# Merge gates of a gated two-branch block by Strassen's products, in a stage ahead of attention

## The chip, the core and the metric

The kernel runs on one core of a Trainium2 chip. The metric is device time in microseconds (us). The engines are called as in the profile: PE (TensorE matmul; PEld its weight loads), DVE (VectorE), ACT (ScalarE), POOL (GpSimd), SP (SyncE, whose queue issues the DMAs).

## The reference

One layer of a streaming encoder on 1024 tokens of width 1024. Everything is float32. Cut to what matters here:

```python
h = rms_norm(x, norm_w) * (1 + scale) + shift
(cq, ckv, k_rope, gate_a, q_b, k_b, v_b, f_b, gate_b,
 mg_a, mg_b) = split(h @ w_in)             # mg_a, mg_b: 1024 columns each
o_a = mla_attention(...)                   # 8 heads, from cq, ckv, k_rope
o_b = fox_attention(...)                   # 8 heads, from q_b, k_b, v_b, f_b
y_a, y_b = o_a * silu(gate_a), o_b * silu(gate_b)
merged = sigmoid(mg_a) * (y_a @ w_branch_a) + sigmoid(mg_b) * (y_b @ w_branch_b)
out = x + gate * (merged @ w_out)
```

## The kernel before

Float32 products are made of three float32r products: each operand is split into a high part (a rounding copy on ACT, L115) and a low part (the rest, a subtraction on DVE, L116), and high x high, high x low and low x high are summed in PSUM. `hT_hi` and `hT_lo` hold h, transposed: 8 tiles of 128 columns by 1024 tokens.

In order of time: phase 0 (h, and the latent cq), latents, the operands of branch A (`g2q`, `g2k`), attention over 16 heads (8 of branch A, 8 of branch B), the branch products, the output product. The order of every engine is the order in which the program emits its instructions; nothing reorders them, so an instruction that waits holds up all behind it on its engine.

Work that only has to be done in time is a generator, `fillers`, from which other stages draw some matmuls at a time with `fill_to(t)`, until a running count of PE time, `pe_time`, reaches t. It yields first `g1b` (q, k, v of branch B, banks `b`, six column chunks b0 to b5 of four units of 48 matmuls), then 24 chunks of 128 columns (`f`, from `w_t`): eight of the SiLU gates, sixteen of the merge gates, each two units of 24 matmuls of 512 tokens; then the branch products. A merge-gate unit goes through a tanh (L1022) and by DMA to `mg_d`.

Attention is one stream (`attention`): per head 12 steps. A step transposes one block of the softmax matrix P (`pt`, `turn`), splits it (`pp`: ACT L1240, DVE L1241), makes the scores of a tile ahead (`s`; mask L1210 or memset L1212, maximum L1214, exponential L1220, reciprocal L1223, scaling on POOL L1224), prepares operands of later heads, draws fill, and multiplies the block of the step before with V (`o`). Each step moves a due time on by `STEP`, and fill is drawn up to it:

```python
for k in range(12):
    due += self.STEP
    pr = self.turn(n, g, j)          # transposes and split of block k
    ...                              # scores ahead, operands ahead
    self.fill_to(due - 600)
    if k not in (1, 5):
        while queue: queue.pop(0)()  # product of the block before
    self.fill_to(due)
    queue.append(pr)
```

SBUF beside the fixed tensors is dealt out in slots by hand (`U`, 29 of 128x1024; `Hs`, 11 of 128x512); a new tile in a slot waits for the last reader of the old one.

Of the kernel before, what the change touches and what calls it, by code (L numbers as in the profile page):

```python
# [41 lines left out]
class Slots:  # L42
    """Equal pieces of SBUF, taken and given back by hand; the one given back longest ago goes first."""
# [31 lines left out]
class Net:  # L75
    STEP = 2490.0
# [6 lines left out]
    # ------------------------------------------------------------ helpers  # L83
    def rsqrt(self, ssq, n, count, tag, between=iter(())):
        """between: other work of the vector engine, for the time each step waits for the one before."""
# [13 lines left out]
    def load_w(self, src, shape, name):  # L99
        """A weight piece in a slot, still whole; split() makes its two parts."""  # L100
        raw = self.U.get(shape, F32, f"raw_{name}")
        self.nc.sync.dma_start(raw, src)
        return raw
# [20 lines left out]
    def mm(self, out, l, r, start, stop):  # L124
        n = int(np.prod(r.shape[1:]))
        self.pe_time += max(4 * n / 2.4, 213.0) if r.dtype == F32 else n / 2.4 + 2
        self.nc.tensor.matmul(out, lhsT=l, rhs=r, start=start, stop=stop)  # L127
# [14 lines left out]
    def fill_to(self, t):  # L142
        """Matmuls off the critical path until the tensor engine is booked up to t."""
# [9 lines left out]
    # ------------------------------------------------------------ constants  # L153
# [84 lines left out]
    # ------------------------------------------------------------ phase 0  # L238
    def phase0(self):
# [46 lines left out]
        def warm(n, src):  # L286
            """Keeps the tensor engine's clock up while it waits for x."""
# [23 lines left out]
        def broadcast_c():  # L311
            """c along the free dimension of every partition, through a diagonal and a product with ones."""
# [15 lines left out]
        def ada_rows(kt, bank):  # L328
            """The shift of a block whose rows lie on the partitions."""
# [193 lines left out]
    # ------------------------------------------------------------ latents  # L523
# [211 lines left out]
    # ------------------------------------------------------------ branch A operands  # L735
# [109 lines left out]
    # ------------------------------------------------------------ work off the critical path  # L845
    def g1b(self, hook):
        """q, k and v of branch B: 256 columns at a time, two token tiles in a bank."""
# [11 lines left out]
        for ci in range(6):  # L859
            kind, half = ci // 2, ci % 2  # L860
            for sp in range(4):
# [4 lines left out]
                if ci == 5 and sp in (0, 2):  # L866
                    hook()
# [58 lines left out]
    def gate_sum(self, chs, engine="d"):  # L926
        """128 columns of the adaLN gate each."""
# [15 lines left out]
    def gate_row(self):  # L943
        """The gate as a row, quartered (the two factors of a half that the merge gates leave out)."""
# [12 lines left out]
    def fillers(self):  # L957
        """All GEMMs that only have to be done in time, some matmuls at a time; True where an accumulation ends."""
        nc, t, U, Hs = self.nc, self.t, self.U, self.Hs
        chunks = [("t", c) for p in range(8) for c in (p, 8 + 2 * p, 9 + 2 * p)]  # L960
# [28 lines left out]
        yield from self.g1b(first)  # L989
# [85 lines left out]
    # ------------------------------------------------------------ attention  # L1075
    # One instruction stream for all heads, in emission order: a step transposes one k block of P and multiplies the one
    # before, and carries the scores of a tile ahead, the operands of the head after next and a share of the gate GEMMs.
    def prep_a(self, n):
        """Operands of heads n and n + 1 of branch A, turned together: rows 0-63 of a transpose are head n's."""
# [207 lines left out]
    def attention(self):  # L1287
# [13 lines left out]
        for c, i in enumerate((0, 4, 1, 5, 2, 3, 6)):  # L1301
            if c == 3:
                self.load_v(1)
            if c == 4:
                while not self.g1b_done:
                    next(self.fill)
# [227 lines left out]
```

## Time and profile before

| | us |
|---|---|
| median of 3 runs (lowest, highest) | 989.82 (989.09, 990.09) |
| span of the profiled execution, first to last instruction | 989.3 |
| branch B's q, k, v end; first attention prologue | 283 to 332 |
| attention, 16 heads | 332 to 835 |
| branch products | 835 to 897 |
| output product | 897 to 989 |

The profile page gives each engine's busy time, the span in 40 slices, the chain of work that ended last, and the costliest groups of instructions. A PE instruction's duration includes its way through the array and overlaps the next one's; what one matmul costs in a row of them is read from the chain of work, as time divided by count.

### The profile page before, as it was taken

What the parts mean: (1) busy time and instruction counts of PE and PEld (TensorE: products, weight loads), DVE (VectorE), ACT (ScalarE), POOL (GpSimd) and SP (SyncE); (2) the same over time, 40 slices, a digit from 0 to 9 for tenths busy, and PEclk for the clock granted to TensorE, in tenths of its full rate; (3) what the DMA queues carried; (4) which work ended last, traced back from release to release, by engine and by line L of the source; (5) the groups of instructions that cost most, each with busy time, mean ns of one, the idle gap of its engine ahead of it and who ended that gap; (6) DMA issues with size and microseconds to landing.
All of it is one profiled execution on the core that took longest, in us unless ns stands there. A gap on an engine that the chain in (4) does not pass through costs nothing.

```text
span 989.3 us, 15335 instructions
## 1 busy us (share of the span) xinstructions
PE 954.5 (96%) x5550; PEld 833.1 (84%) x5550; DVE 659.8 (67%) x1399; ACT 475.7 (48%) x962; POOL 250.8 (25%) x279
## 2 busy tenths in 40 slices
PE   6479999999999999999999999999999999999998
PEld 6379999999998888888888888888888888887887
DVE  6997787676734766757667667677676767495222
ACT  6347653344334655655646566566565644143000
POOL 4843222220001222221223233333332220045000
PEclk9889999999999999999999999999999999999999
DMA  9733113346485223424224232231321554643321
GB/s 345 285 128 131 52 55 107 124 150 221 155 251 149 67 95 84 139 66 109 84 65 119 77 108 66 86 109 65 118 87 45 181 181 148 228 148 126 100 92 64
DMA packets 80700, 123.95 MB, mean 125 GB/s; under 512 B 5896, under 2 KB 47504, under 8 KB 80624
## 3 DMA queue, kind: packets, MB, share of 16 engines
q1 hardware_dynamic: 80624, 122.96, 38.1%
q8 instruction: 44, 0.72, 0.3%
q14 instruction: 32, 0.26, 0.1%
HBM read 87.29 MB, written 35.66 MB: 124 GB/s over the span
## 4 chain that ended last, share of the span: by engine, by line
PE 85%; DVE 8%; DMA 4%; issue 1%; ACT 1%; SPq 0%; POOL 0%; ACTq 0%; DVEq 0%; POOLq 0%
PE f L127 31%; PE b L127 12%; PE out L127 9%; PE s L127 8%; PE o L127 7%; PE pt L136 6%; PE q L127 3%; PE ckv L127 2%; PE kv L127 2%; DVE hT_lo L1046 1%; DVE hT_lo L365 1%; DMA ks_u<-ka_d 1%; DVE wada_u L339 1%; PE cq_s L127 1%; DVE xT L359 1%
## 5 line engine op out<-in xcount | busy, mean ns | idle before, releaser
L1240 ACT CAST pp_u<-pt 128x512 fp32r<-128x512 f32 x192 | 92.1, 480 | 181.6 <-PE pt L136 167.8
L1241 DVE TENSOR_TENSOR pp_u<-pt,pp_u 128x512 fp32r<-128x512 f32 x192 | 106.6, 556 | 79.2 <-ACT pp_u L1240 77.1
L127 PE MATMUL f<-hT_hi,hi_f_u 128*128 128x512 f32 x384 | 153.6, 400 | 0.0
L127 PE MATMUL f<-hT_hi,lo_f_u 128*128 128x512 f32 x384 | 153.4, 400 | 0.0
L127 PE MATMUL f<-hT_lo,hi_f_u 128*128 128x512 f32 x384 | 153.2, 399 | 0.0
L127 PE MATMUL s<-k_u,q_u 96*128 96x512 f32 (+6 forms) x480 | 116.4, 361 | 0.7 <-ACT p_h L1220 0.7
L127 PE MATMUL b<-hi_b_u,hT_hi 128*128 128x256 f32 x384 | 109.6, 285 | 0.0
L127 PE MATMUL b<-hi_b_u,hT_lo 128*128 128x256 f32 x384 | 108.6, 283 | 0.0
L127 PE MATMUL b<-lo_b_u,hT_hi 128*128 128x256 f32 x384 | 108.6, 283 | 0.0
L1224 POOL TENSOR_SCALAR p_u<-p_u,rs 128x640 f32<-128x640 f32 (+1 forms) x64 | 65.2, 1018 | 164.4 <-DVE rs L1223 95.9
L1224 POOL TENSOR_SCALAR p_h<-p_h,rs 128x128 f32<-128x128 f32 (+1 forms) x64 | 38.6, 603 | 245.5 <-DVE rs L1223 205.7
L1214 DVE TENSOR_REDUCE nm<-s 128x1 f32<-128x128 f32 (+7 forms) x128 | 97.0, 758 | 4.4
L127 PE MATMUL o<-pp_u,v_u 128*128 128x512 f32 (+7 forms) x384 | 94.2, 340 | 0.0
L127 PEld LDWEIGHTS f<-hT_hi,lo_f_u 128*128 128x128 f32 x384 | 72.4, 189 | 11.9
L127 PEld LDWEIGHTS f<-hT_lo,hi_f_u 128*128 128x128 f32 x384 | 72.5, 189 | 11.2
L127 PEld LDWEIGHTS f<-hT_hi,hi_f_u 128*128 128x128 f32 x384 | 72.5, 189 | 11.1
L127 PEld LDWEIGHTS s<-k_u,q_u 96*128 96x128 f32 (+2 forms) x480 | 76.7, 190 | 6.1 <-ACT p_h L1220 1.2
L127 PEld LDWEIGHTS o<-pp_u,v_u 128*128 128x128 f32 (+1 forms) x384 | 61.8, 161 | 19.6
L127 PEld LDWEIGHTS b<-lo_b_u,hT_hi 128*128 128x128 f32 x384 | 73.6, 192 | 0.3
L127 PEld LDWEIGHTS b<-hi_b_u,hT_hi 128*128 128x128 f32 x384 | 73.6, 192 | 0.3
L127 PEld LDWEIGHTS b<-hi_b_u,hT_lo 128*128 128x128 f32 x384 | 73.6, 192 | 0.0
L136 PEld LDWEIGHTS pt<-ident,p_u 128*128 128x128 f32 x416 | 52.7, 140 | 16.6
(319 smaller groups left out, 2072.0 us busy)
## 6 DMA issues: line engine op xcount, KB each, us to landing
raw_f_u<-in_w_t SPq DMA_DIRECT2D x24, 512.0 KB
wada_u<-in_w_ada SPq DMA_DIRECT2D x16, 512.0 KB
mg_d<-th_h SPq DMA_DIRECT2D x32, 256.0 KB
mg_h<-mg_d SPq DMA_DIRECT2D x32, 256.0 KB
raw_b_u<-in_w_b SPq DMA_DIRECT2D x12, 512.0 KB
x_u<-in_x SPq DMA_DIRECT2D x8, 512.0 KB
raw_wg_u<-in_w_gate SPq DMA_DIRECT2D x8, 512.0 KB
va_d<-vhl_u SPq DMA_DIRECT2D x8, 512.0 KB
```

The source lines that it names most:

```text
L127: self.nc.tensor.matmul(out, lhsT=l, rhs=r, start=start, stop=stop)
L136: self.nc.tensor.transpose(out=out, in_=in_, identity=self.ident)
L339: nc.vector.scalar_tensor_tensor(out=w, in0=w, scalar=1.0, in1=self.cb, op0=ALU.mult, op1=ALU.mult, accum_out=a)
L359: (nc.vector if engine == "d" else nc.gpsimd).tensor_scalar(out=xT[:, kt, c], in0=xT[:, kt, c], scalar1=gs[:, kt, 1:2], scalar2=gs[:, kt, ...
L365: nc.vector.tensor_tensor(out=lo[:, kt, c], in0=xT[:, kt, c], in1=hi[:, kt, c].bitcast(F32), op=ALU.subtract)
L1046: nc.vector.tensor_tensor(out=self.hT_lo[x], in0=mA[c1][:, x[2]], in1=self.hT_hi[x].bitcast(F32), op=ALU.subtract)
L1214: nc.vector.tensor_reduce(out=nm, in_=sv, axis=AX.X, op=ALU.max, negate=True)
L1224: nc.gpsimd.tensor_scalar(out=p[:, 0:w], in0=p[:, 0:w], scalar1=rs, scalar2=0.0, op0=ALU.mult, op1=ALU.add)
L1240: nc.scalar.copy(ph[:, c0:], pt[:, c0:])
L1241: nc.vector.tensor_tensor(out=pl[:, c0:], in0=pt[:, c0:], in1=ph[:, c0:].bitcast(F32), op=ALU.subtract)
```

## The change

Twelve of the sixteen merge-gate chunks (all of branch A's, four of branch B's) leave the fill. They are done as six pairs of chunks in a new stage, `merge_gates`, between `g2k` and attention. A pair is a product of a 2x2 block matrix of weights (two chunks by two halves of the contraction, A11 to A22) with one of h (two halves of the contraction by two of the tokens, B11 to B22). Winograd's form of Strassen's scheme makes it with seven block products of 12 matmuls instead of eight. It needs sums of blocks: of h once (`token_sums`: T1 to T4, for two tiles of the contraction at a time, p = 0 and 1), of the weights for every pair (`column_sums`: S1 to S4). The sums are made on POOL and split on ACT and DVE. Three PSUM banks (x, y, z) collect the seven products; half-sums are read out of a bank while it goes on collecting.

`g1b` is now drawn to its end before the stage, with the token sums emitted between its units, two steps a unit. The fill of attention is then 12 chunks (eight SiLU gates, four merge gates) and the branch products; `STEP` goes from 2490 to 1700.

```diff
-    STEP = 2490.0
+    STEP = 1700.0
...
-        chunks = [("t", c) for p in range(8) for c in (p, 8 + 2 * p, 9 + 2 * p)]
+        chunks = [("t", c) for p in range(8) for c in (p, *self.plain.get(p, ()))]
...
+    def token_sums(self):
...
+        def parts(nm, p, src):
+            hi, lo = (U.get([P, 2, 512], F32R, f"T{nm}{e}{p}") for e in "hl")
+            nc.scalar.copy(hi, src)
+            nc.vector.tensor_tensor(out=lo, in0=src, in1=hi.bitcast(F32), op=sub)
+            self.T[nm, p] = hi, lo
+
+        for p in range(2):
+            b11, b12, b21, b22 = (quarter(k, t, p) for k in range(2) for t in range(2))
+            a, b = (U.get([P, 2, 512], F32, f"Tsum{p}{e}") for e in range(2))
+            g(out=a, in0=b12[0], in1=b11[0], op=sub)
+            yield
+            g(out=b, in0=b12[1], in1=b11[1], op=sub)
+            yield
+            g(out=a, in0=a, in1=b, op=add)
+            parts("T1", p, a)
+            yield
+            g(out=a, in0=b22[0], in1=a, op=sub)
+            yield
+            g(out=a, in0=a, in1=b22[1], op=add)
+            parts("T2", p, a)
...
+    def merge_gates(self):
...
+        def product(n, left, nm, acc, start):
+            w = ops[n].pop(left)
+            for k in range(4):
+                h, l = right(nm, k)
+                for e, (a, b) in enumerate(((w[:, 0, k], h), (w[:, 0, k], l), (w[:, 1, k], h))):
+                    self.mm(acc, a, b, start and k == 0 and e == 0, k == 3 and e == 2, loose=True)
+            U.put(w)
...
+        for n, (c1, c2) in enumerate(self.pairs):
+            for _ in prep:
+                pass
...
+            product(n, "A11", "B11", x, True)
+            nc.scalar.copy(s1, x)
+            product(n, "S2", "T2", y, True)
+            tt(out=v, in0=y, in1=s1, op=ALU.add)
+            product(n, "S1", "T1", z, True)
+            product(n, "S3", "T3", y, False)
+            tt(out=w, in0=y, in1=s1, op=ALU.add)
+            tt(out=w, in0=z, in1=w, op=ALU.add)
+            gate(c2, 1, w, w)
+            product(n, "A12", "B21", x, False)
+            gate(c1, 0, u, x)
+            product(n, "S4", "B22", z, False)
+            tt(out=v, in0=z, in1=v, op=ALU.add)
+            gate(c1, 1, v, v)
+            self.column_load(n + 2)
+            product(n, "A22", "T4", y, False)
+            tt(out=s1, in0=y, in1=s1, op=ALU.add)
+            gate(c2, 0, s1, s1)
...
-            if c == 4:
-                while not self.g1b_done:
-                    next(self.fill)
-                self.fbanks = "fg"
...
+        self.pairs = [(8 + 2 * p, 9 + 2 * p) for p in range(6)]
+        self.plain = {p: (16 + p,) for p in range(4, 8)}
...
+                sums, n = self.token_sums(), 0
+                while not self.g1b_done:
+                    if next(self.fill):
+                        n += 1
+                        next(sums, None)
+                        next(sums, None)
+                for _ in sums:
+                    pass
+                self.column_load(0)
+                self.first_pair = {}
+                self.first_ops = self.column_sums(0, self.first_pair)
+                next(self.first_ops)
+                next(self.first_ops)
+                self.column_load(1)
+            with tc.tile_pool(name="psw", bufs=1, space=PSUM) as self.psw:
+                self.merge_gates()
+            self.fbanks = "fg"
```

POOL's queue between `g2q` and attention. `Tsum` are the slots a and b of `token_sums`. Before:

```order
L780 TENSOR_TENSOR qraw_u_110_2273<-rp_h_47_2302 128x256
L1224 TENSOR_SCALAR p_0_h_70_3456<-p_0_h_70_3456,rs_0_3488 128x128
L1224 TENSOR_SCALAR p_4_u_161_3487<-p_4_u_161_3487,rs_4_3524 128x640
L1224 TENSOR_SCALAR p_1_h_71_3523<-p_1_h_71_3523,rs_1_3560 128x256
L1224 TENSOR_SCALAR p_5_u_164_3559<-p_5_u_164_3559,rs_5_3596 128x768
```

And now:

```order
L780 TENSOR_TENSOR qraw_u_110_2273<-rp_h_47_2302 128x256
L1096 TENSOR_TENSOR Tsum_u_144_3195<-hT_hi 128x1024
L1098 TENSOR_TENSOR Tsum_u_145_3196<-hT_lo 128x1024
L1100 TENSOR_TENSOR Tsum_u_144_3195<-Tsum_u_144_3195,Tsum_u_145_3196 128x1024
L1103 TENSOR_TENSOR Tsum_u_144_3195<-hT_hi,Tsum_u_144_3195 128x1024
L1105 TENSOR_TENSOR Tsum_u_144_3195<-Tsum_u_144_3195,hT_lo 128x1024
L1108 TENSOR_TENSOR Tsum_u_144_3195<-hT_hi,Tsum_u_144_3195 128x1024
L1110 TENSOR_TENSOR Tsum_u_144_3195<-Tsum_u_144_3195,hT_lo 128x1024
L1113 TENSOR_TENSOR Tsum_u_144_3195<-hT_hi 128x1024
L1115 TENSOR_TENSOR Tsum_u_145_3196<-hT_lo 128x1024
L1117 TENSOR_TENSOR Tsum_u_144_3195<-Tsum_u_144_3195,Tsum_u_145_3196 128x1024
```

Ten sums for p = 0, in two slots; the same ten follow for p = 1 in two others, and then four sums of 128x512 for every pair of chunks, the first pair's directly behind them.

ACT's queue while b5 is computed. `bv` reads a bank of b5's; `TT1h` and the like are the high parts of the token sums, `A_0` the high part of the first pair's A11. Before:

```order
L882 CAST bv_2_u_162_3497<-b_2_3415 128x8x64
L1220 ACTIVATE p_4_u_161_3487,sm_4_3514<-s_4_3477,nm_4_3485 128x640
L1220 ACTIVATE p_1_h_71_3523,sm_1_3547<-s_1_3516,nm_1_3521 128x256
L882 CAST bv_3_u_165_3581<-b_3_3501 128x8x64
L1220 ACTIVATE p_5_u_164_3559,sm_5_3586<-s_5_3549,nm_5_3557 128x768
```

And now:

```order
L880 CAST bv_3_u_146_3248<-b_3_3199 128x8x64
L1089 CAST TT1h_u_147_3253<-Tsum_u_144_3195 128x1024
L880 CAST bv_0_u_149_3307<-b_0_3258 128x8x64
L1089 CAST TT2h_u_150_3312<-Tsum_u_144_3195 128x1024
L880 CAST bv_1_u_152_3366<-b_1_3317 128x8x64
L1089 CAST TT4h_u_153_3371<-Tsum_u_144_3195 128x1024
L880 CAST bv_2_u_155_3425<-b_2_3376 128x8x64
L1089 CAST TT3h_u_156_3431<-Tsum_u_144_3195 128x1024
L880 CAST bv_3_u_158_3484<-b_3_3435 128x8x64
L1089 CAST TT1h_u_161_3494<-Tsum_u_159_3489 128x1024
```

`TT2h`, `TT4h` and `TT3h` of the second half follow, and then the first pair's operands, A11's at their head. The first copy of a token sum stands behind the last bank of b4 (the first row). DVE's low parts stand in the same order. On PE the matmul behind b5's last is the first one of A11 x B11.

PE in one step of head 10 (branch B). Before:

```order
L136 MATMUL pt10_14_7520<-ident_89,p10_7_u21_449_7313 128x128
L127 MATMUL s11_3_7530<-k1_11_u20_417_6861,q1_11_u27_400_6643 128x512
L127 MATMUL s11_3_7530<-k2_11_u14_418_6862,q2_11_u6_401_6644 128x512
L127 MATMUL f17_00_7514<-hT_hi_80,hi_f17_u1_457_7387 128x512
L127 MATMUL f17_00_7514<-hT_lo_81,hi_f17_u1_457_7387 128x512
L127 MATMUL f17_00_7514<-hT_hi_80,lo_f17_u13_458_7388 128x512
L127 MATMUL f17_00_7514<-hT_hi_80,hi_f17_u1_457_7387 128x512
L127 MATMUL f17_00_7514<-hT_lo_81,hi_f17_u1_457_7387 128x512
L127 MATMUL o10_1_7481<-pp10_13_u18_464_7491,v10_u19_428_6993 128x512
L127 MATMUL o10_1_7481<-pp10_13_u18_464_7491,v10_u19_428_6993 64x512
L127 MATMUL f17_00_7514<-hT_hi_80,lo_f17_u13_458_7388 128x512
```

And now:

```order
L136 MATMUL pt10_14_7920<-ident_89,p10_7_u3_503_7744 128x128
L127 MATMUL s11_3_7930<-k1_11_u27_475_7369,q1_11_u12_459_7180 128x512
L127 MATMUL s11_3_7930<-k2_11_u0_476_7370,q2_11_u6_460_7181 128x512
L127 MATMUL f9_10_7869<-hT_lo_81,hi_f9_u23_486_7507 128x512
L127 MATMUL o10_1_7890<-pp10_13_u19_518_7900,v10_u17_483_7470 128x512
L127 MATMUL o10_1_7890<-pp10_13_u19_518_7900,v10_u17_483_7470 64x512
L127 MATMUL f9_10_7869<-hT_hi_80,lo_f9_u25_487_7508 128x512
```

Six fill matmuls became two; transposes, scores and products are the same. Counted over the order, the fill matmuls between the first transpose of head 0 and the last product of head 15 go from 1250 to 546: in a pair of heads of branch A from about 144 to 56, of branch B from 161 to 73. Head 14's first seven steps hold none: the twelve chunks are used up in head 13, and the branch products wait for the outputs of heads 0 to 7 that head 14 loads and splits.

## Rows read from the trace of the kernel before

**Rows 1.** The page: busy time of engines; PE and its clock in 40 slices.

```profile
PE 954.5 (96%) x5550; PEld 833.1 (84%) x5550; DVE 659.8 (67%) x1399; ACT 475.7 (48%) x962; POOL 250.8 (25%) x279
...
PE   6479999999999999999999999999999999999998
...
PEclk9889999999999999999999999999999999999999
```

**Rows 2.** Busy time by stage: attention. Columns: window, length, then each engine.

```profile
core 0: us, PE busy (x) PEld busy (x) DVE busy (x) ACT busy (x) POOL busy (x), PEclk, DMA share, GB/s
332.00:835.00 503.00, 502.75 (x2703) 419.17 (x2702) 344.18 (x717) 291.20 (x623) 136.85 (x166) 1.00 0.32 98
```

**Rows 3.** The chain that ended last, pieces in order: start, us, what.

```profile
265.89 15.13 PE b L127 x126
281.04 0.59 ACT bv_u L882
```

**Rows 4.** The same chain, later: the branch products.

```profile
834.35 16.64 PE f L127 x73
```

**Rows 5.** POOL's two-operand sums by line: duration ns min/median/max, times, shape.

```profile
L342 POOL TENSOR_TENSOR wada_u<-wada_u,cb_u x6: 2386/3155/3329, 27.4 to 47.4; 128x1024 f32<-128x1024 f32 x6
...
L932 POOL TENSOR_TENSOR raw_wg_u<-raw_wg_u,cb_u x4: 2400/2706/3375, 58.3 to 66.5; 128x1024 f32<-128x1024 f32 x4
```

**Rows 6.** Groups by line and shape: copies and subtractions (busy us, mean ns).

```profile
L116 DVE TENSOR_TENSOR lo_f_u<-raw_f_u,hi_f_u 128x512 fp32r<-128x512 f32 x64 | 45.6, 752 | 9.0 <-ACT hi_f_u L115 8.9
L115 ACT CAST hi_f_u<-raw_f_u 128x512 fp32r<-128x512 f32 x64 | 36.5, 622 | 5.6 <-DMA raw_f_u<-in_w_br 5.4
L1220 ACT ACTIVATE p_u<-s,nm 128x1024 f32<-128x1024 f32 x16 | 17.9, 1121 | 5.3 <-DVE nm L1214 5.1
L1214 DVE TENSOR_REDUCE nm<-s 128x1 f32<-128x1024 f32 x16 | 19.6, 1224 | 0.5
```

**Rows 7.** Windows around PE's idle stretch in phase 0, columns as rows 2.

```profile
35.00:40.00 5.00, 2.95 (x21) 2.48 (x19) 4.97 (x3) 3.13 (x6) 5.00 (x3) 1.00 0.74 260
40.00:45.00 5.00, 0.97 (x6) 0.60 (x4) 5.00 (x5) 0.69 (x1) 5.00 (x3) 0.91 0.58 199
45.00:50.00 5.00, 0.00 (x0) 0.00 (x0) 4.97 (x4) 1.59 (x3) 4.78 (x2) 0.50 0.40 113
50.00:55.00 5.00, 4.89 (x15) 4.62 (x16) 4.93 (x10) 2.28 (x3) 0.00 (x0) 0.57 0.00 0
55.00:60.00 5.00, 5.00 (x27) 4.88 (x27) 4.96 (x9) 3.18 (x5) 1.73 (x1) 1.00 0.65 216
```

**Rows 8.** Two pairs of heads, one of each branch, columns as rows 2.

```profile
418.70:483.30 64.60, 64.60 (x354) 54.22 (x352) 43.06 (x93) 37.44 (x81) 15.11 (x19) 1.00 0.34 99
644.20:708.50 64.30, 64.05 (x345) 53.08 (x343) 44.21 (x93) 37.15 (x80) 19.88 (x27) 1.00 0.27 83
```

**Rows 9.** The same two windows, L116 alone: DVE, then POOL.

```profile
418.70:483.30 64.60, 4.55 (x6) 0.00 (x0) 1.00 0.34 99
644.20:708.50 64.30, 3.84 (x6) 0.00 (x0) 1.00 0.27 83
```

**Rows 10.** DVE's groups of a step in attention, by shape (busy us, mean ns).

```profile
L1241 DVE TENSOR_TENSOR pp_u<-pt,pp_u 128x512 fp32r<-128x512 f32 x94 | 64.8, 690 | 40.6 <-ACT pp_u L1240 39.5
L1210 DVE TENSOR_TENSOR s<-s,maskb 128x128 f32<-128x128 f32 x64 | 18.5, 290 | 0.6 <-PE s L127 0.6
L1214 DVE TENSOR_REDUCE nm<-s 128x1 f32<-128x768 f32 x15 | 14.4, 957 | 0.5
L1223 DVE RECIPROCAL rs<-sm 128x1 f32<-128x1 f32 x119 | 18.9, 159 | 17.2 <-ACT p_u L1220 16.1
```

More of the change, by code (lines that the diff above doesn't have):

```diff
@@ L122, in split, with mm @@
         return hi, lo
-    def mm(self, out, l, r, start, stop):
+    def mm(self, out, l, r, start, stop, loose=False):
         n = int(np.prod(r.shape[1:]))
         self.pe_time += max(4 * n / 2.4, 213.0) if r.dtype == F32 else n / 2.4 + 2
-        self.nc.tensor.matmul(out, lhsT=l, rhs=r, start=start, stop=stop)
+        self.nc.tensor.matmul(out, lhsT=l, rhs=r, start=start, stop=stop, skip_group_check=loose)
     def mm3(self, out, lh, ll, rh, rl, start, stop):
@@ L843, in g2k, with g1b @@
         self.store(*items)
-    def g1b(self, hook):
+    def g1b(self):
         nc, t, U, Hs = self.nc, self.t, self.U, self.Hs
@@ L865, in g1b @@
                     w[ci + 1][sp - 1] = self.split(w[ci + 1][sp - 1], f"b{ci + 1}_{sp - 1}")
-                if ci == 5 and sp in (0, 2):
-                    hook()
                 acc = self.fbank(f"b{ci}_{sp}")
@@ L988, in fillers @@
         low, mA = [], {}
-        yield from self.g1b(first)
+        self.fill_first = first
+        yield from self.g1b()
         for pos, (k, u) in enumerate(todo):
@@ L1073, in split_y, with quarter @@
         self.y[4 * br + k] = self.split(self.y[4 * br + k], f"y{br}{k}")
+    def token_sums(self):
+        nc, U = self.nc, self.U
+        self.T = {}
+        g, sub, add = nc.gpsimd.tensor_tensor, ALU.subtract, ALU.add
+        def quarter(k, t, p):
+            x = (slice(None), slice(4 * k + 2 * p, 4 * k + 2 * p + 2), slice(512 * t, 512 * t + 512))
+            return self.hT_hi[x].bitcast(F32), self.hT_lo[x].bitcast(F32)
+        def parts(nm, p, src):
[17 more added lines that the diff above has]
+            parts("T2", p, a)
+            yield
+            g(out=a, in0=b21[0], in1=a, op=sub)
+            yield
+            g(out=a, in0=a, in1=b21[1], op=add)
+            parts("T4", p, a)
+            yield
+            g(out=a, in0=b22[0], in1=b12[0], op=sub)
+            yield
+            g(out=b, in0=b22[1], in1=b12[1], op=sub)
+            yield
+            g(out=a, in0=a, in1=b, op=add)
+            parts("T3", p, a)
+            U.put(a, b)
+            yield
@@ new lines, in column_sums, with parts @@
+    def column_sums(self, n, ops):
+        nc, U, Hs = self.nc, self.U, self.Hs
+        r1, r2 = self.raws.pop(n)
+        a11, a12, a21, a22 = r1[:, 0:4], r1[:, 4:8], r2[:, 0:4], r2[:, 4:8]
+        g, sub, add = nc.gpsimd.tensor_tensor, ALU.subtract, ALU.add
+        def parts(nm, src):
+            o = U.get([P, 2, 4, P], F32R, f"{nm}_{n}")
+            nc.scalar.copy(o[:, 0], src)
+            nc.vector.tensor_tensor(out=o[:, 1], in0=src, in1=o[:, 0].bitcast(F32), op=sub)
+            ops[nm] = o
+        s1, s2 = (Hs.get([P, 4, P], F32, f"s{e}_{n}") for e in (1, 2))
+        g(out=s1, in0=a21, in1=a22, op=add)
+        parts("A11", a11)
+        yield
+        g(out=s2, in0=s1, in1=a11, op=sub)
+        parts("S2", s2)
+        yield
+        parts("S1", s1)
+        g(out=s2, in0=a12, in1=s2, op=sub)
+        Hs.put(s1)
+        yield
+        g(out=a11, in0=a11, in1=a21, op=sub)
+        parts("S3", a11)
+        yield
+        parts("A12", a12)
+        yield
+        parts("S4", s2)
+        Hs.put(s2)
+        yield
+        parts("A22", a22)
+        U.put(r1, r2)
+        yield
@@ L1407, in build @@
         self.pending, self.pending_b = (), ()
+        self.pairs = [(8 + 2 * p, 9 + 2 * p) for p in range(6)]
+        self.plain = {p: (16 + p,) for p in range(4, 8)}
+        self.raws = {}
         self.seq = [("a", h) for h in range(H)] + [("b", h) for h in range(H)]
```

44 lines of the change are left out of this document (added).

## The prediction

> **What bounds the kernel now.** First the page: PE is busy 96% of the span, from the fourth slice to the next to last nine tenths or more, and its clock is full there; no other engine is over 67% [rows 1]. Then attention by itself: PE is busy 502.75 of 503.0 us, DVE 344.2, ACT 291.2, POOL 136.9 [rows 2]. So the time is the sum of what PE does. Busy time says little of one matmul, since they overlap; the chain gives it: 73 matmuls of 512 columns in 16.64 us, 228 ns each [rows 4], and 126 of 256 columns in 15.13 us, 120 ns each [rows 3]. A matmul that goes saves 228 ns, as long as PE finds work without waiting. Two places decide whether it still does: the entrance to the new stage, and attention with thinner fill.
>
> **Removed.** Twelve chunks took 12 x 48 = 576 matmuls; six pairs take 6 x 7 x 12 = 504. 72 x 0.228 = 16.4 us less on PE, each operand still one weight load to one matmul. The rest of the fill only moves: 704 matmuls leave attention's 16 heads (160.5 us), 110 more stand in its prologue, 18 more behind it, 504 in the new stage (115 us). tanh, stores to `mg_d` and weight loads are the same in number; the seven splits of a pair (four were needed before: two halves each of two chunks) cost ACT 7 x 0.62 and DVE 7 x 0.75 us [rows 6], its four POOL sums about 5 us, all of it beside 84 x 0.228 = 19.2 us of matmuls. A pair's operands are made during the pair before it. From the second pair on I cost the stage at its matmuls.
>
> **Added: the way into the stage.** The token sums are one chain. In the order, ten POOL sums of 128x1024 work on one slot a; after the third, fifth and seventh the slot is copied by ACT and subtracted from by DVE, and the next sum overwrites it, so it waits for both; the same for p = 1. The first copy stands on ACT behind the read of b4's last bank, the row of ACT at 281.04 us in this trace, which ends at 281.63 [rows 3]; b5's matmuls before it are unchanged, so it stands there afterwards too. POOL can do only the first three sums ahead of that. From 281.6 on: six waits, each a copy and a subtraction of 1024 elements. The copy is 1.1 to 1.25 us (the exponential of 1024, or two copies of 512), I take 1.15; the subtraction 1.2 to 1.5 (the maximum over 1024, or two of 512), I take 1.3 [rows 6]; 6 x 2.45 = 14.7. Then the last T3's high part, 1.15, and A11's high and low part behind it in the same two queues, 0.62 + 0.75. That is 281.6 + 14.7 + 2.5 = 298.8 us, plus seventeen sums of length t. The rows of that shape run from 2.39 to 3.38 us [rows 5]; the long ones lie where DVE is busy nearly all the time [rows 7], and in this chain DVE mostly works while POOL waits, so I take 2.5, near the shortest. 298.8 + 42.5 = 341.3 us.
>
> PE has b5 behind b4: 281.04 + 192 x 0.120 = 304.1 us, and the next matmul on it is A11 x B11, which needs the last of that chain although it uses no token sum. PE stands from 304.1 to 341.3: **37 us**. Bounds: t = 2.39 gives 35, t = 3.2 gives 49; the other prices move it by 2 either way. Nothing covers it: the fill is not drawn from there, and attention's prologue stands behind the stage.
>
> The Trainium skill prices this: its GPSIMD Engine Reference (Elementwise — side-by-side cycle accounting) gives about 2.6 cycles an element at 1.2 GHz for a sum of two float32 inputs, and has such work go to VectorE, about twice as fast. An estimate from it is 2.2 us a sum, a wait of 32 us and a total 5 us below mine; no row here is that short, the shortest is 2.39.
>
> After such a wait the clock is low: in phase 0 PE idles some nine us, the granted clock falls to 0.50 and is 0.57 over the first 5 us of work [rows 7], that is 1.2 of 2.4 GHz most of the time; 0.43 x 5 = **2 us**. The first pair alone has its operands made while it runs: seven splits and the next pair's A11 stand on ACT ahead of the read of bank x (8 x 0.62 = 5 us, DVE 8 x 0.75 = 6), and the fourth product must wait for the sum that reads bank y. The third product ends 8.2 us in. I put **2 us**, bounds 0 and 4.
>
> **Moved: attention.** 704 matmuls fewer leave PE 503.0 - 160.5 = 342.5 us. DVE loses only the splits of the chunks that left. Per pair of heads, branch A: PE 64.6 - 88 x 0.228 = 44.5; DVE 43.1, less 88/144 of the 4.55 of L116, 40.3 [rows 8, 9]. Branch B: PE 64.3 - 20.1 = 44.2; DVE 44.2 - 88/161 x 3.84 = 42.1. DVE goes from 67 and 69% to 91 and 95% of PE's time. That is an average; a step is tighter. Five steps of a head have a block of 512 and a tile ahead: 0.69 + 0.29 + 0.96 + 0.16 = 2.1 us of DVE [rows 10] against 44.2/24 = 1.84 of PE; two or three light ones have a third of that. PE can lead DVE by about a step, since the product with V waits for the low part and transposes have two banks. If nothing carries over, the five steps lose 5 x 0.26 = 1.3 us a head, and the steps in which operands or a split come on top (1.5 us of DVE, about once in two heads beyond what PE has there) 0.9: 2.2 x 14 heads = 31 us. If all carries over, 0. I take half, **15 us**: a lead of one step evens out neighbours, but dense steps stand in a row.
>
> Head 14 has no fill in its first seven steps. DVE's share of them is about 7/12 of half a pair, 12.3 us; PE's own work there, (64.3 - 161 x 0.228)/2 x 7/12 = 8.0. PE loses 4.3 us, more with the splits of y on DVE: **5 us**, bounds 3 and 10. ACT, at some 33 of 44 us, is not the one that ends last.
>
> **Sum**, against the profiled span of 989.3: -16.4 + 37 + 2 + 2 + 15 + 5 = +44.6, 1033.9. The runs' median is 0.5 above the span: **1034 us**. With all low bounds 989.8 - 16.4 + 33 + 2 + 0 + 0 + 3 = 1011; with all high ones 989.8 - 16.4 + 51 + 2 + 4 + 31 + 10 = 1071.
>
> **Rivals.**
> 1. Attention keeps PE full; only the wait at the entrance is paid. For it: in the kernel before PE waits for nothing there, and DVE's sum is still under PE's. Against: 95% on an engine in order, with dense steps in a row. 989.8 - 16.4 + 37 + 2 + 2 + 3 = 1017.
> 2. DVE sets the pace of attention step by step, and the sums run at the middle of their rows, t = 2.75: 989.8 - 16.4 + 41.5 + 2 + 2 + 31 + 8 = 1058.
> 3. The stage waits in every pair, not in the first alone: token sums hold 16 of the 29 slots, two pairs' operands and loads up to 12, so a split may wait for a product to end. A wait of a product and a half, 4 us a pair, gives 1034 + 24 = 1058. Against: a slot given back is needed only a pair later.
> 4. Faster: no wait at the entrance, attention full, 989.8 - 16.4 + 3 = 976. The point from which it decides is t: seventeen sums would have to fit between 298.8 and 304.1, 0.31 us each, or the sums not stand in a chain. The rows say eight times that, and the order shows the chain.
>
> **How the numbers follow.** Forecast 0.5, rival 1 0.2, rival 2 0.18, rival 3 0.07, rival 4 0.05. The range takes in the forecast's bounds and rivals 1 to 3, without the corner where all high bounds meet: 1008 to 1064. A measurement of this kernel tells apart about 0.2%, 2 us. Only rival 4 is faster, 0.04 of it clearly; the cases end too far above for no change: 0.02; slower 0.94.
>
> **What would show it.** In the changed kernel's trace: b5's last matmul near 304 us, the first of bank x near 341; POOL's twenty L1096 to L1117 sums at about 2.5 us, its idle time among them ended by DVE's low parts; a clock near half for some us behind the wait; six pairs at about 19.3 us each. In attention about 22.5 to 23.5 us a head, PE waiting for DVE (`pp`, `nm`), DVE over 90% busy; head 14 some 5 us longer. The prediction is wrong if PE starts the stage before 325 us, if attention takes under 345 or over 385 us, or if pairs take over 22 us.

## The result, and the profile after

The change makes the kernel slower: 1090.43 us in the median (1085.84 to 1090.91) beside 989.96 (989.09 to 990.18) for the kernel before on the same chip, a ratio of 1.100 (95% interval 1.098 to 1.102). The profiled execution spans 1089.1 us, before 989.3.

The page of the kernel after: busy time of the engines, then PE and its clock in 40 slices.

```profile
PE 971.8 (89%) x5478; PEld 824.5 (76%) x5478; DVE 703.6 (65%) x1455; ACT 501.9 (46%) x994; POOL 328.4 (30%) x323
...
PE   6689999999924999989998989998999869999998
...
PEclk9799999999966999999999999999999989999999
```

PE has fallen from 96% [rows 1] to 89%: a hole in the 12th and 13th slices, the clock with it, from the 18th slice on eights among the nines where before there were nines alone, and a six in the 33rd. The stages of the kernel after by windows (us, then PE, PEld, DVE, ACT, POOL busy with instructions, clock, DMA share, GB/s): b5, the wait, the first pair in two pieces, the five other pairs, attention's prologue, attention, the branch products behind it.

```profile
core 0: us, PE busy (x) PEld busy (x) DVE busy (x) ACT busy (x) POOL busy (x), PEclk, DMA share, GB/s
281.60:305.10 23.50, 23.50 (x197) 23.31 (x195) 6.45 (x7) 5.40 (x7) 15.04 (x7) 1.00 0.25 91
305.10:340.20 35.10, 0.02 (x1) 0.00 (x0) 7.06 (x6) 6.23 (x7) 27.47 (x13) 0.54 0.22 75
340.20:345.00 4.80, 3.58 (x8) 2.39 (x9) 3.68 (x4) 1.14 (x2) 3.35 (x2) 0.50 0.00 0
345.00:364.05 19.05, 18.06 (x79) 14.61 (x78) 11.82 (x15) 9.42 (x16) 7.25 (x6) 0.98 0.21 71
364.05:459.40 95.35, 95.35 (x421) 78.64 (x419) 39.71 (x56) 31.65 (x55) 23.44 (x16) 1.00 0.28 99
459.40:503.50 44.10, 38.99 (x179) 32.13 (x179) 19.87 (x40) 16.55 (x32) 3.15 (x5) 0.96 0.62 134
503.50:932.70 429.20, 385.23 (x2070) 300.47 (x2069) 320.22 (x698) 268.87 (x578) 133.51 (x170) 0.98 0.28 83
932.70:996.90 64.20, 64.18 (x283) 52.81 (x282) 46.45 (x64) 19.91 (x35) 12.99 (x8) 1.00 0.59 204
```

Where the 100 us come from, against the span of before: 72 matmuls fewer -16.4; the entrance +35.1; low clock and first pair +4.3 (119.2 us for the six pairs, 504 x 0.228 = 114.9); attention's prologue +5; attention +73 (429.2, where PE alone needs 516.6 - 704 x 0.228 = 356.1; 516.6 is the time before from head 0's first transpose, at 317.7, to the end of head 15); together about -2 in what lies before the stage and behind attention. In attention PE is busy 90%, before all but 0.25 of 503 us [rows 2], while DVE is busy 75% and ACT 63%: no engine is full.

The 73 us are two things. Heads 0 to 13 take 369.8 us, 26.4 a head, where PE's own work is 22.2 (before: 32.3 with 76.2 fill matmuls a head; now 31.8, and 44.4 x 0.228 = 10.1): 59 us. The same heads before, in a window:

```profile
317.71:769.93 452.22, 451.68 (x2440) 377.22 (x2439) 306.99 (x649) 264.50 (x566) 127.04 (x158) 1.00 0.29 88
```

Heads 14 and 15 lose the other 14. Head 14 takes 36.3 us. A piece of the chain that ended last in it (start, us, what):

```profile
879.00 0.38 SPq L102
879.48 5.05 DMA raw_y_u<-ya_d
884.61 0.63 ACT hi_y_u L115
...
885.87 0.69 DVE lo_y_u L116
886.55 0.60 DVE pp_u L1404
```

The gated outputs of branch A, which heads 0 to 7 stored, are loaded here; a load takes 5.05 us before its split can begin, and no fill is left to run meanwhile. Behind the splits stand attention's own copies on ACT and low parts on DVE. PE's clock falls as well:

```profile
882.00:891.00 9.00, 5.74 (x20) 4.25 (x21) 6.96 (x15) 6.06 (x12) 0.95 (x3) 0.50 0.68 244
```

Four transposes take 1.00 to 1.11 us in this window and 0.60 at the head's start, at a clock of 1.00; by that nearly half of the 5.74 us of busy time, 2 to 3 us of head 14's loss, is the clock (an estimate).

### The profile page after: what moved, and what is told of

Read it like the earlier page. It is cut to its first block, busy times and chain, and to the rows that moved or that the text cites. A ratio compares the mean times of both kernels' runs of the same rounds, so it can differ in the third digit from the quotient of the medians.

```text
span 1089.1 us, 15379 instructions
## 1 busy us (share of the span) xinstructions
PE 971.8 (89%) x5478; PEld 824.5 (76%) x5478; DVE 703.6 (65%) x1455; ACT 501.9 (46%) x994; POOL 328.4 (30%) x323
## 5 line engine op out<-in xcount | busy, mean ns | idle before, releaser
L127 PE MATMUL s<-k_u,q_u 96*128 96x512 f32 (+6 forms) x480 | 118.9, 367 | 12.3 <-ACT p_u L1383 9.1
L1387 POOL TENSOR_SCALAR p_u<-p_u,rs 128x640 f32<-128x640 f32 (+1 forms) x64 | 62.3, 973 | 142.9 <-DVE rs L1386 81.0
L127 PE MATMUL o<-pp_u,v_u 128*128 128x512 f32 (+7 forms) x384 | 97.2, 348 | 2.3 <-DVE pp_u L1404 2.3
L136 PE MATMUL pt<-ident,p_u 128*128 128x128 f32 x416 | 73.2, 284 | 18.5 <-DVE pp_u L1404 9.4
L1387 POOL TENSOR_SCALAR p_h<-p_h,rs 128x128 f32<-128x128 f32 (+1 forms) x64 | 35.8, 559 | 178.0 <-DVE rs L1386 170.6
L127 PE MATMUL f<-hT_hi,hi_f_u 128*128 128x512 f32 x192 | 79.3, 413 | 1.3 <-DVE ws_h L1232 1.3
L127 PE MATMUL f<-hT_hi,lo_f_u 128*128 128x512 f32 x192 | 78.8, 411 | 0.0
L127 PE MATMUL f<-hT_lo,hi_f_u 128*128 128x512 f32 x192 | 78.1, 407 | 0.0
L1383 ACT ACTIVATE p_u<-s,nm 128x640 f32<-128x640 f32 (+1 forms) x64 | 61.2, 957 | 28.8 <-DVE nm L1377 23.1
L127 PE MATMUL wx<-hT_hi,A_u 128*128 128x512 f32 x96 | 33.1, 407 | 36.3 <-ACT A_u L1131 35.1
```

Of the source, the lines that this page charges most:

```text
L136: self.nc.tensor.transpose(out=out, in_=in_, identity=self.ident)
L1383: nc.scalar.activation(p[:, 0:w], sv, AF.Exp, bias=nm, accum_out=sm)
L1387: nc.gpsimd.tensor_scalar(out=p[:, 0:w], in0=p[:, 0:w], scalar1=rs, scalar2=0.0, op0=ALU.mult, op1=ALU.add)
```

## Experiments

### Thin fill alone, without the stage

The kernel before with plain products throughout; only the allowance of a step and the order of the chunks are changed:

```diff
-    STEP = 2490.0
+    STEP = 1700.0      # 2100.0, 2300.0
...
-        chunks = [("t", c) for p in range(8) for c in (p, 8 + 2 * p, 9 + 2 * p)]
+        chunks = [("t", c) for p in range(8) for c in (p, 16 + p)[:1 + p // 4]]
+        chunks += [("t", c) for c in range(8, 20)]
```

With 1700: 

> The kernel before, all products plain, no new stage; only the step's time allowance goes from 2490 to 1700 and the merge-gate chunks are put behind the SiLU gates' and four of their own, so that heads 0 to 12 hold the same fill, matmul for matmul, as in the changed kernel (26 to 39 a head instead of 69 to 83); the rest of the fill follows attention. PE's work is that of before. Theory (attention itself cannot go faster, its own round trips between PE, ACT, DVE and POOL set the pace with thin fill): 14 to 15 heads lose 4.3 us each as in the changed kernel, 989.9 + 60 to 65 = 1050 to 1055, heads at 24.5 to 28 us. Rival (the loss comes from what the stage leaves behind: slots, stores of the gates, loads): attention keeps PE full, 989 to 1000. The prediction's half-loss: 1005.

With 2100: 

> The same as the kernel with 1700, with a step's allowance of 2100: 48 to 61 fill matmuls a head. Theory of a fixed pace of about 26.4 us a head: PE's own sum is there 22.1 + 21 x 0.228 = 26.9 us, so nearly nothing is lost, 990 to 997. Rival (every round trip costs its stall whatever the fill around it): 4.3 us a head as with 1700, 1050. A mixture, half the loss: 1020.

With 2300: 

> The kernel before, all products plain, with an allowance of 2300 a step: 59 to 74 fill matmuls a head, 66 in the mean, as if two pairs of chunks had left attention. PE's own sum is 29.8 us a head. If thin fill costs only below a fixed pace (26 us): 989.9 to 992. If the loss falls off gradually (4.1 us a head at 32 matmuls, 1.4 at 53): 0.4 to 0.7 a head, 996 to 1001, more than the 5.5 us that two pairs by seven products save.

Windows over heads 0 to 13 (columns as above), 1700:

```profile
318.74:685.24 366.50, 333.85 (x1824) 258.58 (x1823) 282.62 (x621) 238.56 (x514) 123.91 (x158) 1.00 0.26 72
```

2100:

```profile
319.13:717.03 397.90, 389.00 (x2136) 318.88 (x2135) 296.07 (x635) 251.04 (x539) 126.23 (x158) 1.00 0.28 83
```

2300:

```profile
316.92:742.00 425.08, 420.18 (x2292) 348.85 (x2291) 301.89 (x641) 257.65 (x553) 123.29 (x158) 1.00 0.29 86
```

| allowance | fill a head | us a head | PE's own | lost a head | median us | ratio (interval) |
|---|---|---|---|---|---|---|
| 2490 (before) | 76.2 | 32.3 | 32.3 | 0 | 989.96 | 1 |
| 2300 | 65.6 | 30.4 | 29.9 | 0.5 | 999.07 | 1.008 (1.006 to 1.010) |
| 2100 | 54.5 | 28.4 | 27.4 | 1.1 | 1008.1 | 1.016 (1.013 to 1.019) |
| 1700 | 32.1 | 26.2 | 22.2 | 3.9 | 1051.46 | 1.060 (1.057 to 1.063) |

(PE's own: 32.3 less 0.228 for every fill matmul that is gone. The ratios are to the kernel before on the same chip, which took 992.0 beside 1700 and 2100 and 991.57 beside 2300.) With 1700, 3.9 of the 4.2 us a head are there without stage, sums or seven products: the loss is attention's own doing. Over these heads the mean clock was 1.00 with 1700 and 0.99 in the changed kernel. With 1700 head 14, which holds fill again, takes 27.0 us. With 2100 neither story of the expectation held, not the fixed pace and not the full loss, nor half of it: a quarter of the loss is there. With 2300 the time is the one expected of a gradual loss. Fill covers attention's waits gradually, and already at 66 matmuls a head some of the cover is missing.

### What sets attention's pace

Five kernels from the changed one. Two take work from DVE, one takes both, two add an instruction of 128x128 to every step, which nobody reads.

```diff
# without P's low part; the product reads the high part twice
-        nc.vector.tensor_tensor(out=pl[:, c0:], in0=pt[:, c0:], in1=ph[:, c0:].bitcast(F32), op=ALU.subtract)
...
# short maximum
-        nc.vector.tensor_reduce(out=nm, in_=sv, axis=AX.X, op=ALU.max, negate=True)
+        nc.vector.tensor_reduce(out=nm, in_=self.ident[:, 0:P], axis=AX.X, op=ALU.max, negate=True)
-            nc.scalar.activation(p[:, 0:w], sv, AF.Exp, bias=nm, accum_out=sm)
+            nc.scalar.activation(p[:, 0:w], sv, AF.Exp, bias=nm, scale=1.0 / 16, accum_out=sm)
# more work, behind the low part: on ACT, or on DVE
+        nc.scalar.copy(self.extra_tile, self.ident)
+        nc.vector.tensor_tensor(out=self.extra_tile, in0=self.ident, in1=self.ident, op=ALU.add)
```

Short maximum: 

> The changed kernel with every maximum over the scores replaced by one over 128 columns of a constant tile (and the scores scaled by 1/16 in the exponential, so that nothing overflows): the softmax is another one, the instructions, their order and all waits but the maximum's length are the same. It takes 8 x 0.758 - 8 x 0.29 = 3.7 us of DVE a head away, and shortens the way from scores to exponential by up to 0.9 us a tile. If DVE's work sets the pace (throughput or round trip): heads 0 to 12 from 26.4 to 23 to 24 us, time 1090.4 - 13 x 2.9 = 1050 or below. If ACT and POOL do: heads at 26, time 1085 to 1090.

No low part: 

> The changed kernel without the low part of P: the 192 subtractions on DVE are left out and the second product of a block reads the high part, so P has the precision of one part; PE's work is the same in number. It takes 6.6 us of DVE a head away and frees a transposition bank at ACT's copy. If DVE's in-order work sets the pace: heads 0 to 12 at 22.5 to 23.5 us, time about 1045. If the round trip through the score bank sets it, whose DVE part (mask, maximum) is left: heads at 25 to 26, time 1070 to 1080.

Both: 

> Both cuts at once: the changed kernel without the low part of P (the second product reads the high part) and with every maximum over 128 columns of a constant tile (scores scaled by 1/16), so the softmax is another one. Alone the first took 1.9 us off each of heads 0 to 13 (26.4 to 24.5), the second 1.6 (24.8), of the 4.3 above PE's own 22.1. If they shorten different waits (PE's wait for the transposition bank and for the score bank), the gains add: heads at 22.9, time 1038 to 1045. If they shorten the same one, heads stay at 24.3 to 24.5 and the time at 1057 to 1060.

More on ACT: 

> The changed kernel with a copy of 128x128 on ACT behind every high part of P (192 in all, about 0.26 us each, 3.1 us a head); nobody reads it. ACT is busy 63% of attention. Theory of DVE's throughput: ACT has room, heads stay at 26.4, time 1090 to 1093. Theory of a round trip in which every engine waits for the other in order: a part of it comes through, some 1 to 1.6 us a head, time 1105 to 1117.

More on DVE: 

> The changed kernel with an addition of 128x128 on DVE behind every low part of P (192 in all, 0.2 to 0.29 us each, about 3 us a head); nobody reads it. Theory of DVE's throughput: it comes through in full, heads at 29.4, time 1090.4 + 48 = 1138. Theory of a round trip: 0.3 to 0.45 of it as in the two cuts, some 1.0 to 1.4 us a head, time 1105 to 1113.

Heads 0 to 13 of the changed kernel, then each of the five in the order above, in windows (columns as before):

```profile
503.46:873.29 369.83, 334.90 (x1818) 260.56 (x1817) 279.11 (x617) 237.65 (x512) 121.87 (x158) 0.99 0.26 74
```

```profile
499.55:847.06 347.51, 325.61 (x1819) 259.56 (x1817) 218.17 (x615) 234.66 (x512) 121.28 (x158) 1.00 0.27 79
```

```profile
500.29:843.91 343.62, 322.25 (x1819) 260.14 (x1818) 198.52 (x449) 236.20 (x512) 122.34 (x158) 1.00 0.28 80
```

```profile
500.62:827.81 327.19, 318.13 (x1819) 260.51 (x1817) 136.67 (x447) 234.31 (x512) 121.32 (x158) 1.00 0.29 84
```

```profile
499.35:871.30 371.95, 334.86 (x1819) 259.35 (x1818) 278.41 (x617) 270.76 (x680) 122.09 (x158) 1.00 0.25 74
```

```profile
500.70:892.97 392.27, 338.71 (x1818) 259.30 (x1817) 330.97 (x784) 236.98 (x512) 124.74 (x158) 1.00 0.24 70
```

| | DVE or ACT work a head | us a head | change | median us |
|---|---|---|---|---|
| changed kernel | | 26.4 | | 1090.4 |
| short maximum | DVE -4.4 | 24.8 | -1.6 | 1060.8 |
| no low part | DVE -5.8 | 24.5 | -1.9 | 1059.7 |
| both | DVE -10.2 | 23.4 | -3.1 | 1042.2 |
| 192 copies more | ACT +2.4 | 26.6 | +0.15 | 1091.2 |
| 192 additions more | DVE +3.7 | 28.0 | +1.6 | 1111.0 |

(Work a head: the differences of the busy columns, by 14.) What is put on DVE, or taken away, moves the time by 0.30 to 0.43 of itself; what is put on ACT at this place costs 0.06 of itself. So DVE's queue is in the path for a third of its work and more, and the length of ACT's queue hardly. Each single cut came out between what its two stories expected, both cuts together as expected of gains that add. The copies on ACT fit the theory of DVE's throughput, in which ACT has room; but by that theory the additions on DVE would have come through in full, 29.4 us a head, and the 28.0 us and 1111.0 that were measured are nearer the theory of a round trip, by which the copies would have cost 1 to 1.6. Neither theory held for both. The two cuts add up, nearly (3.1 of 3.5): the short maximum takes PE's waits for the exponential from 9.5 to 1.9 us, and without the low part its waits for `pp` on DVE, 11.0 us, go. Without both, 1.2 of the 4.2 us are left.

How can an engine that is busy 75% set the pace? Some of the waits of DVE in heads 0 to 13 of the changed kernel, and the first of the kernel before (who, for whom: total us, times, longest):

```profile
DVE rs L1386 <- ACT p_u L1383: 20.4, 35, 0.8
DVE pp_u L1404 <- ACT pp_u L1403: 14.4, 26, 1.8
DVE k_u L1324 <- ACT k_u L1319: 12.2, 8, 1.9
```

```profile
DVE pp_u L1241 <- ACT pp_u L1240: 68.0, 80, 1.8
```

All its waits come to 83 us, 79 of them for ACT. With the 279 us of work that is 362 of 369.8, or 98%. It would be easy to read this as a full queue, but the same sum is 98% in the kernel before, where PE loses nothing (307 of work and 137 of waits, of 452), and 99% without low part and long maximum (137 and 188, of 327). An engine that takes its instructions in order is at work or waiting nearly all the time in any of these kernels, so the sum does not tell which engine limits. How the waits change does. The 52 us added on DVE lengthen the heads by 22; DVE's waits shrink from 83 to 54 us and take up the other 29. The 33 us added on ACT lengthen them by 2; ACT's waits shrink from 128 to 97. DVE has some room, then, and ACT enough for nearly all of it. PE's waits, the same stretch:

```profile
PE s L127 <- ACT p_u L1383: 6.9, 14, 1.1
PE pt L136 <- DVE pp_u L1404: 6.5, 10, 2.0
PE pt L136 <- DVE k_u L1324: 4.2, 6, 1.0
...
PE pt L136 <- POOL p_u L1387: 2.8, 8, 0.5
```

Each of these stands at the end of a way through several engines: a block goes from PE to ACT's copy, DVE's low part and back to PE, the scores from PE to DVE's maximum and ACT's exponential before their bank is free. That the loss is the length of these round trips, with too little fill beside them, is the reading that fits all five kernels; it is argued from the waits. The copy, the exponential and POOL's scaling were not made longer or shorter themselves, so what each is worth stays open (PE's waits for POOL come to 3.5 us). Of the 59 us, 35 are idle time of PE in the trace (369.83 - 334.90); the other 24 lie inside its busy time and are not taken apart here.

### Are banks missing?

Three kernels with one fill bank (`f`) instead of two in attention: with nothing else, with two wide score banks, with three transposition banks.

```diff
-            self.fbanks = "fg"
+            self.fbanks = "f"
...
# two score banks
-        s = self.bank("n" if i < 4 else "s", f"s{n}_{i}")
+        s = self.bank("s", f"s{n}_{i}")
-            self.bufs["s"] = 1
+            self.bufs["s"] = 2
# three transposition banks
-        pt = self.bank("t", f"pt{n}_{g}{j}")
+        self.tturn = getattr(self, "tturn", -1) + 1
+        pt = self.bank("ttg"[self.tturn % 3], f"pt{n}_{g}{j}")
```

Score banks: 

> The changed kernel with two wide score banks in attention instead of one wide and one narrow; the second fill bank is given up for it, so the fill is spaced out, 62 fill matmuls fewer are drawn in the prologue and head 14 holds fill again. If the round trip through the one wide bank (scores, maximum on DVE, exponential on ACT, next scores) sets attention's pace: PE's waits for the exponential (28 us as stamped) go, heads 0 to 12 fall from 26.4 to about 24.5 us. If P's own way (transposition, copy, low part, scaling on POOL) or DVE's order sets it, heads stay at 26 or above. Head 14 falls from 36 to about 27 in both. Time: 1090.4 - 9 (head 14) - 26 = 1055 by the first, 1075 to 1082 by the second.

Transposition banks: 

> The changed kernel with three banks for the transposes of P instead of two; the third is the second fill bank, so fill before attention and in head 14 is as in the kernel with two score banks. If PE's lead over DVE, limited by the transposition banks, sets the pace: the waits of pt for pp's low part (24 us as stamped) go, heads 0 to 12 fall from 26.4 to about 24.7 us, time 1055 to 1060. If it is the score bank: heads at 26 or above, time 1075 to 1082.

One fill bank: 

> The changed kernel with one fill bank in attention instead of two and nothing in the place of the second: what the kernels with two score banks (heads 0 to 13 at 26.2 us) and with three transposition banks (26.9) have in common. If one fill bank alone costs nothing, heads stay at 26.4 and head 14 falls to 27: 1080 to 1090; then neither bank sets the pace. If it costs what a bank gives back, heads are at 27.5 or above and both banks were worth 0.6 to 1.3 us a head.

PE's waits in heads 0 to 13 with two score banks:

```profile
PE f L127 <- DVE gate_u L1025: 6.3, 8, 1.3
PE pt L136 <- DVE k_u L1324: 4.7, 5, 1.3
```

And with three transposition banks:

```profile
PE s L127 <- ACT p_u L1383: 14.3, 13, 1.8
PE o L127 <- DVE pp_u L1405: 4.7, 8, 1.1
```

Heads 0 to 13 in windows: two score banks, three transposition banks, one fill bank alone.

```profile
498.31:864.67 366.36, 330.84 (x1823) 259.99 (x1822) 282.25 (x620) 238.87 (x514) 124.68 (x158) 1.00 0.26 72
```

```profile
498.79:875.38 376.59, 338.79 (x1824) 268.73 (x1823) 282.24 (x620) 238.54 (x514) 123.95 (x158) 0.97 0.25 70
```

```profile
496.53:873.29 376.76, 340.28 (x1823) 266.89 (x1822) 282.53 (x620) 238.83 (x514) 123.82 (x158) 0.97 0.25 70
```

Each bank removes the wait that it was meant for (PE's for the exponential; the transposes' for the low part), and waits come back elsewhere: with two score banks the longest, 6.3 us, is at the one fill bank that is left (2.0 with one fill bank alone), with three transposition banks it is that for the exponential, 14.3 us (12.1 with one fill bank alone). Heads: 26.2, 26.9 and, with the fill bank alone, 26.9 us; medians 1089.4, 1104.9 and 1101.9. None of the three totals is an expected one. Some 8.3 to 10.1 us of each are a wait for the load of the first keys, in attention's prologue, out of which 62 fill matmuls have gone; and 26.9 us with one fill bank lies between the two stories of its expectation. The last two kernels ran at a mean clock of 0.97 in this stretch, the first at 1.00; 3% of 377 us is 11 us (an estimate), as much as the 0.7 us a head between them makes, so I don't credit the second score bank with all of it. Neither bank sets the pace: at most 0.7 of the 4.2 us a head. The Trainium skill (Perfetto Trace Analysis, Optimization Strategy) says that a gap repeating on the engine that should be saturated can mean too little PSUM for the next tile. Read that way, a third transposition bank would help; the measurement says that here it moves the gap.

### The entrance

The changed kernel with the twelve chunks done as plain products in the same place (no sums), and the changed kernel with the token sums on DVE:

```diff
# plain stage: for the four (chunk, half) of a pair
+                for kt in range(KT):
+                    self.mm3(acc, h[:, kt], l[:, kt], self.hT_hi[:, kt, sl], self.hT_lo[:, kt, sl], kt == 0, kt == KT - 1)
...
# sums on DVE, in token_sums
-        g, sub, add = nc.gpsimd.tensor_tensor, ALU.subtract, ALU.add
+        g, sub, add = nc.vector.tensor_tensor, ALU.subtract, ALU.add
```

Plain: 

> The changed kernel with the stage in its place, but its twelve chunks done as plain products (96 matmuls a pair of chunks instead of 84), without token sums and sums of the weights. If the wait at the entrance comes from the token sums alone, it goes: 1090.4 - 35.1 - 2 (low clock behind it) - 1 (first pair) + 72 x 0.228 = 1069, between 1065 and 1073, with attention at 429 us as before. If attention's loss hangs on what Strassen's form leaves behind (slots, operands), attention falls towards 360 and the time to 1000 to 1030. If the wait is that of a loaded operand, it stays: 1106.

On DVE: 

> The changed kernel with the twenty token sums on DVE instead of POOL. Theory (chain of 17 sums behind the first copy sets the stage's start): a sum of 128x1024 on DVE at 1.3 to 1.5 us (two subtractions of 512 columns) instead of POOL's, start of the stage at 319 to 325 instead of 340.2 us, total 1069 to 1076. Rival (the stage waits for something else, a load or the copies on ACT): 1088 to 1092.

1070.6 us (ratio 1.0785, 1.075 to 1.082) and 1071.7 us (1.0795, 1.076 to 1.083); heads at 26.3 and 26.6 us. Both totals lie in the range expected, but their parts do not. In the plain stage PE's wait was expected to go and shrinks from 35.1 to 8.5 us, which are a load and a split that this kernel issues late; the 72 matmuls come back. On DVE a sum takes 1.22 us instead of POOL's 2.34 to 2.4, and PE's wait is 23.2 us, longer than the 14 to 20 I had put: on one queue sum, copy on ACT and subtraction follow each other too, with 1.1 us of DVE waiting at every copy. The stage starts 11.5 us earlier than in the changed kernel, yet head 0 starts 18.4 us earlier (485.0 and 503.5): 5.6 of it lies in attention's prologue, where this execution lacks a wait for a load that the changed kernel's trace has (below). That the total fits is in part luck. The Trainium skill (GPSIMD Engine Reference, Elementwise — side-by-side cycle accounting) puts GpSimd's sum at twice VectorE's time; 2.34 to 1.22 agrees.

## Why the prediction was wrong

- **Matmuls and pairs**: right. 504 matmuls at 228 ns; the five pairs behind the first in 95.4 us with PE full (19.1 each; put at 19.3). Rival 3, a wait in every pair, falls.
- **The way into the stage**: right. b5 ends at 305.1 (304.1), the first product starts at 340.2 (341.3), the hole is 35.1 (37). The chain is the one described, in the timeline of the kernel after (start, us, what, idle before and who ended it):

```profile
330.23 1.23 DVE L1090 TENSOR_TENSOR TT4l_u<-Tsum_u,TT4h_u 128x1024 fp32r<-128x1024 f32 x1 [5.94 <-ACT TT4h_u L1089]
331.53 2.34 POOL L1113 TENSOR_TENSOR Tsum_u<-hT_hi 128x1024 f32<-128x1024 f32 x1 [2.41 <-DVE TT4l_u L1090]
...
338.61 1.05 ACT L1089 CAST TT3h_u<-Tsum_u 128x1024 fp32r<-128x1024 f32 x1 [8.42 <-POOL Tsum_u L1117]
339.56 0.61 ACT L1131 CAST A_u<-raw_mg_u 128x512 fp32r<-128x512 f32 x1
...
340.23 0.79 PE L127 MATMUL wx<-hT_hi,A_u 128*128 128x512 f32 x1 [35.11 <-ACT A_u L1131]
```

  A sum alone took 2.34 to 2.41 us (2.5 was taken, the shortest row was 2.39), a handover 2.41 (2.45); one sum took 3.32 (last section). The first product waited for A11's high part alone, not for the low part as the sum has it (0.75); PE waited 1.2 us for that within the pair. The prediction's estimate from the Trainium skill (GPSIMD Engine Reference, Elementwise — side-by-side cycle accounting), 2.2 us a sum, was a little short.
- **Clock and first pair**: right, 4.3 us for all six pairs (2 + 2). The first pair took 23.8 us, of which PE waited 2.2.
- **Attention's term**: the step that failed. It put 15 us on heads 0 to 13, with 0 and 31 as bounds; 59 were measured, beyond the upper bound. What it had right is that PE would come to wait for DVE's results with thinner fill. What it had wrong is the price: it let PE lose only what DVE's busy time of a step has over PE's (2.1 us against 1.84 in five dense steps, and the steps with operands on top), 2.2 us a head at most, and took half of that. The runs contradict the rule, not only its size. With the short maximum (0.26 us), or without the low part, a dense step takes about 1.4 us of DVE, well under PE's 1.84; by the rule only the steps with operands, 0.9 us a head, could then lose, but 2.6 and 2.3 were lost. With both cuts DVE is busy 137 of 327 us, and 1.2 were lost. With the allowance of 2100 PE's own work, 27.4/12 = 2.28 us a step, is more than DVE's 2.1 in a dense one, and 1.1 were lost. The sign that the prediction named, DVE over 90% busy, did not come: 75%. In its place the runs show a loss of 4.2 us a head that depends on the fill (0.5, 1.1 and 3.9 with 66, 55 and 32 matmuls a head) and on DVE's work by 0.30 to 0.43 of it: PE waits for results that go through ACT and DVE in turn, and the fill covers these waits or does not. How the loss divides among the stations of that way stays open. The half taken off, for PE's lead, has no support either: with a third transposition bank, which is more lead, heads took the same 26.9 us as with one fill bank alone.
- **Attention's window**: the recorded 503.0 us run from 332 us, but the count of 1250 fill matmuls, from which the 704 come, starts with head 0's first transpose, at 317.7. PE's own time from there is 356.1 us and not 342.5. The sum goes by differences and is not touched by it, and 429.2 us is far over the 385 that were to show the prediction wrong.
- **Head 14**: the cause was right (no fill in its first steps), the size not: 5 us put, 10 as the bound; head 14 alone is 13 us over PE's own 23.4. The working counted DVE's share of the steps, not the load of y, 5.05 us before a split, nor the clock of 0.50 behind it. With fill it takes 27.0 us.
- **Attention's prologue**: +5 us for which there was no term. 3.9 of them are one wait of PE for the load of the first keys. The five kernels that differ from the changed one in attention's DVE and ACT work have the same stage ahead of it; in their traces this wait is 0 to 0.7 us, and head 0 starts at 499.4 to 500.7 us instead of 503.5. Most of the 5 us belongs to this execution, then, and not to the change; what held the load up in it stays open.
- **Rivals**: 1 (attention full) and 4 (faster) fall. Rival 2 came nearest, with DVE's steps setting the pace, but its 1058 us needed sums at 2.75 us and used the same rule and its bound of 31.

Forecast +44.6, measured +100: attention is 53 of the 55 us between them (heads 0 to 13 44, heads 14 and 15 9).

None of the runs points to a version faster than the kernel before. By estimate, the changed kernel without entrance, low clock and head 14's loss would be at 1090 - 35 - 4 - 13 = 1038. Taking two pairs alone out of attention leaves about the fill of the allowance of 2300, whose 0.5 us a head, 7 in all, is more than the 2 x 12 x 0.228 = 5.5 that two pairs save; such a kernel was not run.

## What to carry to other kernels

Work that only has to be done in time is cover for the stage it runs in. Before it is moved out, don't compare busy times alone: here DVE's work of a dense step was 1.4 us with the short maximum, against 1.84 of PE, and 2.6 us a head were lost all the same. Busy time and waits together don't tell it either; that sum was 98% for DVE both when PE was full and when it was not. Small trials do. Thin the fill alone first: one constant and the order of the chunks gave 3.9 of the 4.2 us a head here (26.2 us a head) without any of the new code. Then add a little work to one engine at a time, or take some away, and see how much of it comes through. The Trainium skill (Perfetto Trace Analysis, Optimization Strategy) says that interleaving stretches whose busiest engine differs may improve performance; here, taking them apart cost 59 us over fourteen heads, which agrees.

## What the hardware showed beside

DVE and POOL, each with two inputs in SBUF, seem to have held each other up where they met. Timeline of the kernel after:

```profile
306.74 2.34 POOL L1096 TENSOR_TENSOR Tsum_u<-hT_hi 128x1024 f32<-128x1024 f32 x1
...
307.89 2.27 DVE L1090 TENSOR_TENSOR TT3l_u<-Tsum_u,TT3h_u 128x1024 fp32r<-128x1024 f32 x1 [7.18 <-ACT TT3h_u L1089]
309.04 3.32 POOL L1098 TENSOR_TENSOR Tsum_u<-hT_lo 128x1024 f32<-128x1024 f32 x1
```

DVE's subtraction took 2.27 us (1.23 alone), to about 1.1 us behind the end of POOL's sum; POOL's next sum took 3.32 (2.34 alone). It looks as if each ran only when the other had ended.

In attention with thin fill the clock can fall too. With one fill bank, windows of 3 us:

```profile
523.00:526.00 3.00, 1.16 (x9) 0.92 (x9) 2.90 (x7) 1.56 (x3) 0.91 (x1) 0.96 0.26 81
526.00:529.00 3.00, 2.69 (x6) 2.17 (x7) 1.57 (x4) 1.32 (x4) 1.01 (x1) 0.50 0.46 133
529.00:532.00 3.00, 3.00 (x10) 2.30 (x8) 1.34 (x2) 0.00 (x0) 0.00 (x0) 0.50 0.00 0
532.00:535.00 3.00, 3.00 (x19) 2.61 (x18) 1.25 (x5) 2.03 (x7) 0.83 (x1) 0.90 0.00 0
```

After a window in which PE worked 1.16 of 3 us, the granted clock was 0.50, 1.2 of 2.4 GHz, for about six microseconds, though PE was busy again.
